# Memory projection steps ahead of the last natural block, x loads ordered across two chunks, and an mLSTM step split off, in a one-core encoder layer

## The chip, the core and the metric

The kernel is one program on one core of a Trainium2 chip. A core has a matrix engine (TensorE, PE in the profile, its weight loads PEld), three engines for elementwise work (VectorE: DVE, ScalarE: ACT, GpSimd: POOL) and SyncE (SP), which here only asks for transfers. Transfers between the chip's memory and the core's on-chip memory run on 16 DMA engines beside them. ScalarE asks for some transfers as well, in its own order of instructions, so one that must wait holds up the work behind it.

The metric is device time in microseconds (us) of one execution, as a median over several.

## The reference

One encoder layer over a sequence of 2048 rows of 1024 numbers, with 256 rows of memory, all in 32-bit floats. Cut to what matters here:

```python
u = rms_norm(h) ; proj = u @ w_in                     # 3600 columns
hy = short_conv(proj[:, :1536])                       # Hyena group, 512 channels
y_hy = group_norm(hyena(hy, spec))                    # two long convolutions by FFT
qk = silu(short_conv(proj[:, 1536:2560]))             # mLSTM group, 4 heads x 128
v, o_pre, gates = proj[:, 2560:3072], proj[:, 3072:3584], proj[:, 3584:]
y_ml = group_norm(sigmoid(o_pre) * (mlstm(qk, v, gates, forward) + mlstm(..., backward)))
h = h + concat(y_hy, y_ml) @ w_out
q = rms_norm(h) @ wq ; k = rms_norm(mem) @ wk ; v = rms_norm(mem) @ wv
h = h + softmax(q k^T / 16) v @ wo                    # 4 heads of 256
h = h + relu(rms_norm(h) @ w1)^2 @ w2 ; return rms_norm(h)
```

The kernel folds the attention's weights into the memory side: for each head it computes keys as (wq of the head) times (the head's k) and values as (the head's v) times (wo of the head), once, ahead of the attention.

## The kernel before, in words

**Tiling.** Wide products are formed as three matmuls of split operands (`mm3`, high and low parts, lines 354, 357 and 358 inside one helper). Splitting means a ScalarE cast for the high part and a VectorE subtraction for the low part (line 365). x is scaled, transposed, split and held for 1024 positions at a time (`xh`, `xl`), as two chunks of 512 positions; `hf` 0 and 1 are the two halves of the sequence.

**Order.** The program is written as generators that are woven. Each `yield` hands the turn over; `chain`, `take`, `among` and `beside_each` set which generator goes next, and `weave` compares the work done in two of them. A scheduler then reorders instructions within each engine by a planner's estimates of readiness, so the text sets the priority and not the exact place.

**The projection.** `sweep(cols, hf, ...)` computes the convolved column tiles (Hyena channels, q, k) transposed, one tile of 256 columns after another. `natural(hf, tiles)` computes v, o and the gates in their natural layout: for each tile of 256 columns (272 with the gates) eight row blocks t of 128 positions, each 24 matmuls, an eviction by ScalarE into a tile `st` and a store asked for by ScalarE into `od` or `vd` (lines 851 and 852). Weights come as `wn` and are split into `wh` and `wl`.

**x.** `x_chunk(c)` makes one chunk of x in four pieces of two row groups: load `xt` (line 518, on SP), scale (DVE, line 507), split (ACT and DVE, line 365). In `prep_x` two such chunks follow each other, and each asks for its first piece when it begins. A `pop` after each row block advances them. The last tile of `natural(1, ...)` starts it at t = 4, since the second half of the row blocks no longer needs the columns of the first chunk.

**The memory side.** `prep_mem` loads the transposed memory and scales it, and starts `raw_stream`, which asks for the weights of wk, wq, wv and wo in the tags `wl` and `wh` (tile `wm`, line 414; two halves of 128 x 1024 words for each) and keeps up to four in flight. `memproj` has eight steps. `project` (line 674) makes a head's k or v from the memory and copies it into `kt` (ACT, line 676). `keys` (line 691, steps 0 to 3) multiplies by wq, copies each piece into a staging tile `o` (ACT, line 681) and stores it as `gd` (asked for by ACT, line 693). `values` (line 703, steps 4 to 7) multiplies by wo, with the store `vw` (line 705). Step n issues `project` n + 1 ahead of `keys` or `values` n.

**The mLSTM.** `states` runs the backward scan and stores the state of each of 16 chunks (line 1154 on PE, `cbd`). `mlstm` then runs the chunks forward: `loads(n)` (q, k, backward state, v; line 1215 and 1138 on SP; rows of gates shuffled by DVE at line 1232), `scores(n)` (PE line 1241; POOL adds masks at line 1248, ACT takes exponentials at line 1250 and DVE multiplies at line 1251), values (PE lines 1279 and 1281), the state's update (PE line 1154, DVE line 1160), and after each second chunk a normalisation over the pair (lines 212 to 220 and 1313). Its tables `rows` (line 1210) take the on-chip memory that x held, so they can be loaded only when the last `natural` has read x.

**Program.** The stretch in question is the end of the projection: sweep columns, `natural(0, (0, 1))`, sweep columns 6 and 7, `natural(0, (2,), p.prep_mem, 2)`, then `take(n, 2)` (two steps of `memproj`), then `beside_each(n, take(m, 6))` (a memory step, an mLSTM step, and so on). All of it is woven with `hyena`, whose last part is back products (lines 943 and 985), inverse steps (lines 177 and 190, which read `zg` and `hy` tiles loaded at lines 927 and 930), and stores. Behind it `attention` starts with 16 transposes (line 1415); the rest of the mLSTM's chunks is woven into it. 

Of the kernel before, what the change touches and what calls it, by code (L numbers as in the profile page):

```python
# [10 lines left out]
F32 = mybir.dt.float32  # L11
# [9 lines left out]
D = 1024  # L21
# [112 lines left out]
class Prog:  # L134
# [270 lines left out]
    def raw_stream(self, pool):  # L405
        q, items = [], list(self.mem_items)

        def load():
            w, n = items.pop(0)
            kt = w.shape[0] // 128  # L410
            t = pool.tile([128, kt, n], F32, tag=("wl", "wh")[len(items) % 2], name="wm", bufs=2)
            for k0 in range(0, kt, kt // 2):
                src = w[128 * k0:128 * k0 + 64 * kt].rearrange("(k p) c -> p k c", p=128)
                self.nc.sync.dma_start(out=t[:, k0:k0 + kt // 2], in_=src)
            q.append(t)

        load()
        load()
        yield
        while q:  # L420
            while items and len(q) < 4:
                load()
            yield q.pop(0)

    def inproj_open(self, es):
# [27 lines left out]
        items += [tr[c] for c in (4, 5, 8, 9)] + nat[:2] + tr[6:8] + nat[2:3]  # L453
        self.items, self.mem_items = items, mem

    def inv_rms(self, dst, src):
        nc, sb, n = self.nc, self.isb, dst.shape[1]
# [60 lines left out]
        self.nc.sync.dma_start(out=t, in_=src[:, 2 * j:2 * j + 2, 512 * c:512 * c + 512])  # L518
# [12 lines left out]
    def x_first(self):  # L531
        nc, sb = self.nc, self.isb
# [91 lines left out]
    def opened(self):  # L624
        self.xes.close()
        return
        yield

    def turned_in(self):
        self.xin.close()  # L630
        return
        yield

    def prep_x(self, hf):
        self.prepq = chain(self.x_chunk(2 * hf), self.x_chunk(2 * hf + 1))

    def prep_mem(self):
        sb = self.isb
        self.memt = [sb.tile([128, 1088], F32, tag="P", name="mt", bufs=2)[:, 0:D].rearrange("p (k t) -> p k t", k=4)
                     for h in range(2)]  # L640
        self.mst = self.raw_stream(sb)
        next(self.mst)

# [15 lines left out]
    def memproj(self):  # L659
# [8 lines left out]
        def project():  # L668
            w = next(self.mst)
            p = self.mm().rearrange("p (k t) -> p k t", k=2)  # L670
            for m in range(2):
                ms = slice(128 * m, 128 * m + 128)
                for k in range(8):
                    mul(p[:, m], w[:, k, ms], mt[k // 4][:, k % 4], start=k == 0, stop=k == 7)  # L674
            t = sb.tile([128, 4, 256], F32, tag="xn", name="kt", bufs=2)[:, 0:2]
            nc.scalar.copy(t, p)
            return t

        def staged(p):
            o = sb.tile([128, 2, 256], F32, tag="st", name="o", bufs=3)  # L680
            nc.scalar.copy(o, p)
            return o

# [142 lines left out]
    def natural(self, hf, tiles, after=None, at=4):  # L826
        nc, a, sb = self.nc, self.a, self.isb
        xh, xl = self.xh, self.xl
        win = a["w_in"][0]
        for c2 in tiles:  # L830
            n = 256 if c2 < 3 else 272
            c0 = 2560 + 256 * c2
            wh, wl = next(self.wst)
# [347 lines left out]
    def mlstm(self, es):  # L1181
# [824 lines left out]
def program(p):  # L2006
    with ExitStack() as ms:
        with ExitStack() as es:
# [11 lines left out]
            weave(s, f, 140, 102, True)  # L2020
            p.gates_open(es)
            n = p.memproj()
            m = p.mlstm(ms)
            with ExitStack() as hs:
                rest = chain(s, p.sweep(range(4, 10), 1, True), p.natural(1, (3, 0, 1, 2), lambda: p.prep_x(0)),
                             p.natural(0, (3,)), among(p.sweep((4, 5, 8, 9), 0, False), p.gates(), 2),
                             among(chain(p.natural(0, (0, 1)), p.sweep((6, 7), 0, False),
                                         p.natural(0, (2,), p.prep_mem, 2)), p.states(), 1),
                             p.turned_in(), take(n, 2), beside_each(n, take(m, 6)))
                weave(rest, p.hyena(hs), 499, 297, True)  # L2030
            for _ in rest:
                pass
# [10 lines left out]
            p.ffn()  # L2043


def among(g, h, every):
    for i, v in enumerate(g):
        yield v
        if i % every == every - 1:
            next(h, None)  # L2050
    for _ in h:
        pass

# [45 lines left out]
```

## Time and profile before

| what | value |
|---|---|
| median of 3 runs | 3133.62 us (3127.82 to 3135.12) |
| the profiled execution | 3131.11 us, span 3129.0 us |
| mean granted TensorE clock | 0.989 |
| HBM read, written | 401.79 MB, 202.41 MB, 193 GB/s over the span |
| x for the first half's sweep is made at | 643 to 692 us |
| `natural(0, (2,))` on TensorE | 1002 to 1036 us |
| first memory projection, last value product | 1036.7 us, 1211.1 us |
| first transposes of the attention | 1233.6 us |
| mLSTM scores begin (chunks 0 to 5) | 1114.5, 1138.4, 1169.7, 1188.4, 1204.5, 1214.9 us |

A row of the profile's timeline gives the start, the duration, the engine and line, the tiles (out<-in), and in brackets how long the engine sat idle ahead of it and what ended that. `PE ... [7.53 <-ACT xh L365]` reads: TensorE did nothing for 7.53 us until ScalarE's cast on line 365 was done. Names that end in q (SPq, ACTq) are an engine's issue of a transfer. A row of windows gives the busy time of each engine in that stretch, the number of instructions, the granted clock of TensorE (1.00 is full), the share of the 16 DMA engines in use, and GB/s.

### The profile page before, as it was taken

How to read it: one execution, taken by the hardware profiler on the slowest of the kernel's cores; microseconds unless marked ns; L12 is line 12 of the kernel's file. 1: busy time of each engine (PE TensorE's matmuls, PEld its weight loads, DVE VectorE, ACT ScalarE, POOL GpSimd, SP SyncE). 2: the span in 40 equal slices, each digit the busy share in tenths (PEclk: the TensorE clock that was granted, in tenths of full speed). 3: DMA queues.
4: the chain of work that ended last, by engine and by line, in shares of the span. 5: the costliest groups of instructions: out<-in, count | busy, mean ns of one | idle time of the engine just before them, and what ended most of it. 6: DMA issues, size and time to landing. Idle time of an engine off the chain costs nothing.

```text
span 3129.0 us, 42943 instructions
## 1 busy us (share of the span) xinstructions
PE 3029.1 (97%) x14257; PEld 2374.5 (76%) x14257; DVE 1964.8 (63%) x3448; ACT 1489.6 (48%) x2907; POOL 1146.9 (37%) x802
## 2 busy tenths in 40 slices
PE   8999999989999898999999999999999999999998
PEld 6655667766677666888887888888888878888876
DVE  7965466446646456777674656657545686555695
ACT  5443366533656225555544455556555533333335
POOL 0122012200113244324141337766456393434493
PEclk9999999999999999999999999999999999999999
DMA  6464767666878897455375657657644574434324
GB/s 212 153 210 163 235 203 220 194 215 216 241 206 249 261 316 245 145 190 186 127 268 186 217 166 243 207 178 231 205 152 153 179 234 142 152 123 152 122 91 172
DMA packets 444101, 607.07 MB, mean 194 GB/s; under 512 B 38494, under 2 KB 248542, under 8 KB 442856
## 3 DMA queue, kind: packets, MB, share of 16 engines
q1 hardware_dynamic: 405988, 546.54, 54.3%
q10 hardware_dynamic: 37892, 57.79, 5.3%
q8 instruction: 113, 1.85, 0.2%
q14 instruction: 108, 0.88, 0.1%
HBM read 401.79 MB, written 202.41 MB: 193 GB/s over the span
## 4 chain that ended last, share of the span: by engine, by line
PE 81%; DMA 7%; DVE 6%; ACT 3%; issue 2%; POOL 1%; SPq 0%; ACTq 0%; DVEq 0%; POOLq 0%
PE mm L354 17%; PE mm L358 17%; PE mm L357 17%; PE hy L358 5%; PE hy L354 5%; PE hy L357 5%; PE hy L177 3%; PE mm L912 1%; PE hy L943 1%; PE hy L985 1%; DMA xt<-in_x_t_dram 1%; DVE bl L1623 1%; PE mm L674 1%; DMA a<-hy 1%; PE mm L703 1%
## 5 line engine op out<-in xcount | busy, mean ns | idle before, releaser
L1623 DVE TENSOR_TENSOR bl<-wr,bh 128x512 fp32r<-128x512 f32 x213 | 239.8, 1132 | 132.5 <-ACT bh L1622 132.3
L1622 ACT CAST ah<-w 128x512 fp32r<-128x512 f32 x284 | 176.9, 624 | 302.5 <-PE hy L357 155.8
L365 DVE TENSOR_TENSOR wl<-wn,wh 128x512 fp32r<-128x512 f32 (+1 forms) x300 | 217.6, 772 | 102.7 <-ACT wh L365 102.4
L354 PE MATMUL mm<-xh,wh 128*128 128x512 f32 x640 | 267.7, 419 | 12.2 <-ACT wh L365 9.1
L990 POOL TENSOR_TENSOR b<-b,a 128x512 f32<-128x512 f32 x64 | 87.0, 1362 | 510.1 <-ACT b L988 320.0
L357 PE MATMUL mm<-xl,wh 128*128 128x512 f32 x640 | 255.8, 400 | 0.7 <-DVE xl L365 0.6
L1622 ACT CAST bh<-wr 128x512 fp32r<-128x512 f32 x232 | 143.8, 622 | 234.6 <-PE mm L358 176.2
L358 PE MATMUL mm<-xh,wl 128*128 128x512 f32 x640 | 255.0, 399 | 0.0
L1623 DVE TENSOR_TENSOR al<-w,ah 128x512 fp32r<-128x512 f32 x236 | 217.6, 922 | 54.9 <-ACT ah L1622 54.9
L358 PE MATMUL mm<-bh,al 128*128 128x512 f32 x576 | 224.1, 392 | 6.8 <-DVE al L1623 4.3
L354 PE MATMUL mm<-bh,ah 128*128 128x512 f32 x576 | 225.7, 392 | 0.5 <-DVE acc L1780 0.4
L357 PE MATMUL mm<-bl,ah 128*128 128x512 f32 x576 | 224.9, 390 | 0.0
L365 ACT CAST wh<-wn 128x512 fp32r<-128x512 f32 (+1 forms) x300 | 167.4, 620 | 110.4 <-PE mm L358 52.1
L357 PE MATMUL mm<-act,wh 128*128 128x512 f32 x512 | 200.5, 393 | 0.8 <-DVE act L365 0.8
L354 PE MATMUL mm<-act,wh 128*128 128x512 f32 x512 | 198.4, 393 | 1.1 <-ACT wh L365 0.9
L358 PE MATMUL mm<-act,wl 128*128 128x512 f32 x512 | 199.1, 392 | 0.3 <-DVE wl L365 0.3
L354 PE MATMUL hy<-bh,ah 128*128 128x512 f32 x448 | 175.2, 391 | 0.0
L357 PE MATMUL hy<-bl,ah 128*128 128x512 f32 x448 | 174.6, 390 | 0.0
L358 PE MATMUL hy<-bh,al 128*128 128x512 f32 x448 | 174.4, 390 | 0.0
L354 PEld LDWEIGHTS mm<-xh,wh 128*128 128x128 f32 x640 | 121.4, 190 | 67.6 <-issue 19.0
L354 PE MATMUL mm<-wh,xh 128*128 128x256 f32 (+1 forms) x512 | 155.7, 305 | 13.0 <-ACT xh L365 10.6
L336 POOL TENSOR_TENSOR b<-b 128x512 f32<-128x512 f32 x32 | 58.3, 1822 | 277.8 <-DVE b L333 137.2
(369 smaller groups left out, 8285.4 us busy)
## 6 DMA issues: line engine op xcount, KB each, us to landing
wr<-hc SPq DMA_DIRECT2D x224, 256.0 KB
w<-in_ff_w_dram SPq DMA_DIRECT2D x172, 256.0 KB
hc<-wn SPq DMA_DIRECT2D x128, 256.0 KB
wn<-in_w_in_dram SPq DMA_DIRECT2D x100, 256.0 KB
hc<-q SPq DMA_DIRECT2D x96, 256.0 KB
fs<-a SPq DMA_DIRECT2D x32, 512.0 KB
a<-fs SPq DMA_DIRECT2D x64, 256.0 KB
a<-zs SPq DMA_DIRECT2D x64, 256.0 KB
```

The lines of the kernel that those rows point to most:

```text
L177: b = self.nc.tensor.matmul(*products[-1], start=True, stop=True)
L336: nc.gpsimd.tensor_tensor(e[1], f, b, ALU.subtract)
L354: first = mm(ps, lh, rh, start=start, stop=False)
L357: mm(ps, lh, rl, start=False, stop=False)
L358: self.last = mm(ps, ll, rh, start=False, stop=stop)
L365: both = (self.nc.scalar.copy(hi, src), self.nc.vector.tensor_tensor(lo, src, hi.bitcast(F32), ALU.subtract))
L674: mul(p[:, m], w[:, k, ms], mt[k // 4][:, k % 4], start=k == 0, stop=k == 7)
L703: mul(p, t[:, m, ms], o_[:, m, ds], start=m == 0, stop=m == 1)
L912: nc.tensor.matmul(pp, dm[:, m], t[:, m], start=True, stop=True)
L990: nc.gpsimd.tensor_tensor(xt, xt, hi[:, m], ALU.mult)
L1622: self.nc.scalar.copy(hi, src)
L1623: eng.tensor_tensor(lo, src, hi.bitcast(F32), ALU.subtract)
```

## The change

Four edits.

1. `x_chunk` becomes `x_chunks`: both chunks of a half run through one list of eight pieces; the first two loads are asked for when the object is made, and the load of piece n + 2 right after piece n is scaled. The last tile of `natural(1, ...)` makes the object at t = 0 and still starts its pieces at t = 4. The first stage uses it as well.
2. Three of the nine turns of `memproj` run ahead of `natural(0, (2,))`: projection 0, then projection 1 with keys 0, then projection 2 with keys 1. `prep_mem` is called in the last sweep column. The weights of `natural(0, (2,))` are made inside `raw_stream` when its fourth weight is handed out, and how many weights it keeps in flight becomes a small table.
3. The memory is scaled in place in its load tiles, `kt` takes a slot of the tag `P`, and the staging tiles `o` alternate between the tags `st` and `cv`.
4. `mlstm` yields once between its first loads and its first scores, and the program takes that step ahead of one more memory step, and then `take(m, 5)` in place of `take(m, 6)`.

```diff
 # raw_stream
         yield
+        n = 0
         while q:
-            while items and len(q) < 4:
+            n += 1
+            if n == 4:
+                self.late_w = iter([self.weights(pool, *self.late_item, kc=2, nbufs=4)])
+            while items and n != 3 and len(q) < {2: 4, 4: 1, 5: 2}.get(n, 4):
                 load()
             yield q.pop(0)
...
-    def x_chunk(self, c):
-        rb = self.spread(self.diagonal(self.rx[:, 4 * c:4 * c + 4]))
-        xs = [self.x_load(c, 0)]
-        for j in range(4):
-            if j < 3:
-                xs.append(self.x_load(c, j + 1))
-            to = slice(2 * j, 2 * j + 2), slice(512 * (c % 2), 512 * (c % 2) + 512)
-            self.scaled(xs.pop(0), 2 * j, self.g_mix, rb, *(t[(slice(None),) + to] for t in (self.xh, self.xl)))
-            yield
+    def x_chunks(self, hf):
+        parts = [(2 * hf + i, j) for i in range(2) for j in range(4)]
+        xs = [self.x_load(*p) for p in parts[:2]]
+
+        def steps():
+            rb = None
+            for n, (c, j) in enumerate(parts):
+                if j == 0:
+                    rb = self.spread(self.diagonal(self.rx[:, 4 * c:4 * c + 4]))
+                to = slice(2 * j, 2 * j + 2), slice(512 * (c % 2), 512 * (c % 2) + 512)
+                self.scaled(xs.pop(0), 2 * j, self.g_mix, rb, *(t[(slice(None),) + to] for t in (self.xh, self.xl)))
+                if n < 6:
+                    xs.append(self.x_load(*parts[n + 2]))
+                yield
+        return steps()
...
     def prep_x(self, hf):
-        self.prepq = chain(self.x_chunk(2 * hf), self.x_chunk(2 * hf + 1))
+        self.prepq = self.x_chunks(hf)
...
-            xs = [load(h) for h in range(2)]
+            xs = self.memt = [load(h) for h in range(2)]
...
-            t = sb.tile([128, 4, 256], F32, tag="xn", name="kt", bufs=2)[:, 0:2]
+            t = sb.tile([128, 1088], F32, tag="P", name="kt", bufs=2)[:, 0:512].rearrange("p (m t) -> p m t", m=2)
...
         def staged(p):
-            o = sb.tile([128, 2, 256], F32, tag="st", name="o", bufs=3)
+            turns[0] += 1
+            if turns[0] % 2:
+                o = sb.tile([128, 2, 256], F32, tag="st", name="o", bufs=3)
+            else:
+                o = sb.tile([128, 1088], F32, tag="cv", name="o", bufs=2)[:, 0:512].rearrange("p (i t) -> p i t", i=2)
...
 # natural
-                if t == at and c2 == tiles[-1] and after is not None:
-                    after()
+                if c2 == tiles[-1] and after is not None:
+                    if t == 0:
+                        nxt = self.x_chunks(0)
+                    if t == at:
+                        self.prepq = nxt
...
 # mlstm
         ld, stores = [loads(0), loads(1)], []
+        yield 1
         scores(0, ld[0])
...
 # program
-            m = p.mlstm(ms)
+            m, st = p.mlstm(ms), p.states()
...
-                             among(chain(p.natural(0, (0, 1)), p.sweep((6, 7), 0, False),
-                                         p.natural(0, (2,), p.prep_mem, 2)), p.states(), 1),
-                             p.turned_in(), take(n, 2), beside_each(n, take(m, 6)))
+                             among(chain(p.natural(0, (0, 1)), p.sweep((6, 7), 0, False, p.prep_mem), take(n, 3),
+                                         p.natural(0, (2,), wst=p.late())), st, 1),
+                             p.turned_in(), take(m, 1), take(n, 1), beside_each(n, take(m, 5)))
```

How this moves instructions, at three places. In each row stand the line, the operation, the tiles (out<-in), the shape and, where a row stands for several instructions, their count. The lines of the changed kernel are some twenty higher.

ScalarE where chunk 1 of x is split (`xh<-xt`) between the evictions `st` of the natural block and their stores `od`; first before:

```order
L503 COPY rb<-mm 128x512
L365 COPY xh<-xt 128x2x512
L851 ACTIVATE st<-mm 128x256
L852 DMA od<-st 128x256
L851 ACTIVATE st<-mm 128x256 x2
L852 DMA od<-st 128x256 x2
L365 COPY xh<-xt 128x2x512
L955 COPY a<-hy 128x512 x2
```

And now:

```order
L507 COPY rb<-mm 128x512
L365 COPY xh<-xt 128x2x512 x2
L871 ACTIVATE st<-mm 128x256 x3
L872 DMA od<-st 128x256 x3
L975 COPY a<-hy 128x512 x2
L365 COPY xh<-xt 128x2x512
```

The second split after the broadcast `rb` stood behind three evictions and three stores; it now stands ahead of them.

TensorE around `natural(0, (2,))` (its matmuls read `wh` and `xh`), first where the block ended before and the memory's projections (`mt,wm`) and keys (`kt,wm`) began:

```order
L358 MATMUL mm<-wh,xl 128x256
L1154 MATMUL hy<-va,kn 128x129 x4
L674 MATMUL mm<-mt,wm 128x256 x14
L1154 MATMUL hy<-va,kn 128x129 x4
L674 MATMUL mm<-mt,wm 128x256 x2
L177 MATMUL hy<-a,e_2618 64x512
L190 MATMUL hy<-a,e_2618 64x512
```

Now, with projection 2 and keys 1 in front of the block (`xt` is the memory, scaled in place):

```order
L685 MATMUL mm<-xt,wm 128x256 x16
L708 MATMUL mm<-kt,wm 128x256
L963 MATMUL hy<-b,em 128x512
L708 MATMUL mm<-kt,wm 128x256 x3
L963 MATMUL hy<-b,em 128x512
L1174 MATMUL hy<-va,kn 128x129 x4
L708 MATMUL mm<-kt,wm 128x256 x12
L354 MATMUL mm<-wh,xh 128x256
L357 MATMUL mm<-wl,xh 128x256
L358 MATMUL mm<-wh,xl 128x256
```

Three projections and two sets of keys moved from behind the natural block to its front, beside the Hyena's back products (`b,em`).

TensorE at the last value products of the memory (`wm,kt`), before, at the end of chunk 3 of the mLSTM (chunk 4 follows, then the transposes):

```order
L703 MATMUL mm<-wm,kt 128x512 x4
L1279 MATMUL hy<-va,rw 128x129
L1281 MATMUL hy<-cbn,rw 128x129
L1279 MATMUL hy<-va,rw 128x129
L1281 MATMUL hy<-cbn,rw 128x129
L1154 MATMUL hy<-ve,kn 128x129 x4
L1241 MATMUL hy<-qn,kk_t 128x128 x4
```

And now, at the end of chunk 0 (chunks 1, 2 and 3 follow, then the transposes):

```order
L1300 MATMUL hy<-va,rw 128x129
L1302 MATMUL hy<-cbn,rw 128x129
L1174 MATMUL hy<-ve,kn 128x129 x4
L720 MATMUL mm<-wm,kt 128x512 x2
L1261 MATMUL hy<-qn,kk_t 128x128 x4
L1300 MATMUL hy<-va,rw 128x129
L1302 MATMUL hy<-cf,rw 128x129
```

The memory's last product stands three chunks earlier in the mLSTM's order than before, and chunk 4 is left to the attention.

More of the change, by code (lines that the diff above doesn't have):

```diff
@@ L452, in inproj_open @@
         items = tr[:4] * 2 + tr[4:] + [nat[c] for c in (3, 0, 1, 2, 3)]
[L453 to L454 removed]
+        items += [tr[c] for c in (4, 5, 8, 9)] + nat[:2] + tr[6:8]
+        self.items, self.mem_items, self.late_item = items, mem, nat[2]
     def inv_rms(self, dst, src):
@@ L627, in opened, with late @@
         yield
+    def late(self):
+        yield next(self.late_w)
     def turned_in(self):
@@ L824, in sweep_out, with natural @@
                 nc.sync.dma_start(out=self.d_kn[t0 + s0:t0 + s0 + rest, cc], in_=st[0:rest, 0])
-    def natural(self, hf, tiles, after=None, at=4):
+    def natural(self, hf, tiles, after=None, at=4, wst=None):
         nc, a, sb = self.nc, self.a, self.isb
@@ L832, in natural @@
             c0 = 2560 + 256 * c2
-            wh, wl = next(self.wst)
+            wh, wl = next(self.wst) if wst is None else next(wst)
             for t in range(8):
@@ L2022, in program @@
             n = p.memproj()
[L2023 removed]
+            m, st = p.mlstm(ms), p.states()
             with ExitStack() as hs:
[L2025 removed]
+                rest = chain(s, p.sweep(range(4, 10), 1, True), p.natural(1, (3, 0, 1, 2), True),
                              p.natural(0, (3,)), among(p.sweep((4, 5, 8, 9), 0, False), p.gates(), 2),
[L2027 to L2029 removed]
+                             among(chain(p.natural(0, (0, 1)), p.sweep((6, 7), 0, False, p.prep_mem), take(n, 3),
+                                         p.natural(0, (2,), wst=p.late())), st, 1),
+                             p.turned_in(), take(m, 1), take(n, 1), beside_each(n, take(m, 5)))
                 weave(rest, p.hyena(hs), 499, 297, True)
@@ L2043, in program, with among @@
             p.ffn()
-def among(g, h, every):
+def among(g, h, every, times=1):
     for i, v in enumerate(g):
@@ L2049, in among @@
         if i % every == every - 1:
-            next(h, None)
+            for _ in range(times):
+                next(h, None)
     for _ in h:
```

3 lines of the change are left out of this document (1 added, 2 removed).

## The prediction

> **What bounds the kernel now.** I read the page's busy table first, then TensorE's waits summed by what ended them, then TensorE's idle time and clock over the three stretches that the change touches.
>
> ```profile
> PE 3029.1 (97%) x14257; PEld 2374.5 (76%) x14257; DVE 1964.8 (63%) x3448; ACT 1489.6 (48%) x2907; POOL 1146.9 (37%) x802
> PE mm L691 <- ACT o L681: 12.9, 2, 10.5
> PE mm L354 <- ACT xh L365: 12.2, 4, 7.5
> PE hy L1279 <- DVE bry L217: 7.5, 2, 5.8
> ```
>
> TensorE is busy for 97%, so about 100 us is all that any reordering can win back. Three waits (total, times, longest) stand near the top of what there is: the memory keys behind their output copies, the natural projection behind the split of x, and the mLSTM's values behind a normalisation. Each belongs to a stage that this change reorders. Elsewhere the same instructions run.
>
> The profiled execution took 3131.11 us (span 3129.0). The median of the three runs is 3133.62, so 2.5 us is added at the end to a sum that is made against the profiled one.
>
> **Part 1, x asked for earlier: -7 us.** Chunk 0 of x is split while the last tile of natural(1) runs; its pieces turn into TensorE work as they come.
>
> ```profile
> 673.77 0.59 PE L354 MATMUL mm<-wh,xh 128*128 128x272 f32 x1 [7.53 <-ACT xh L365]
> 691.19 0.40 PE L354 MATMUL mm<-wh,xh 128*128 128x272 f32 x1 [3.06 <-ACT xh L365]
> 665.47 1.41 DVE L507 SCALAR_TENSOR_TENSOR xt<-xt,par,rb 128x512 f32<-128x512 f32 x2 [4.55 <-DMA xt<-in_x_t_dram]
> 670.05 0.66 ACT L851 ACTIVATE st<-mm 128x256 f32<-128x256 f32 x2 [9.33 <-DMA a<-zg]
> 672.67 1.05 ACT L365 CAST xh<-xt 128x1024 fp32r<-128x1024 f32 x1 [1.96 <-DMA wn<-in_w_in_dram]
> 688.64 1.42 DVE L507 SCALAR_TENSOR_TENSOR xt<-xt,par,rb 128x512 f32<-128x512 f32 x2 [3.12 <-DMA xt<-in_x_t_dram]
> 681.80 0.38 SPq L518 DMA_DIRECT2D xt<-in_x_t_dram  x1
> 670.00:675.00 5.00, 1.23 (x4) 0.95 (x4) 2.12 (x4) 2.19 (x4) 0.00 (x0) 0.50 0.84 286
> ```
>
> The piece is scaled by 665.47 + 1.41 = 666.9, yet ScalarE splits it only at 672.67: an eviction's store stands ahead of it in ScalarE's order, and the row at 670.05 shows 9.33 us lost there. In the new order this split stands ahead of the evictions and their stores. It could then run at about 667 and not 672.67, so some 5 of the 7.53 us go. The last piece was asked for at 681.80 and arrived at 688.64, 6.8 us later, and TensorE idled 3.06 us for it. In the new order its load stands ahead of one gate store, and each load follows its free buffer: 2 of the 3.06 us go. The window's granted clock was 0.50 after the idle 7.53 us, so another 1 to 3 us of slow matmuls may leave with it, and I count none in full. Against that, the first two loads stand where they stood in the queue's order, and the load behind the 665.47 row (asked for at 655.79, 9.7 us) sits in a stretch where the DMA share is 1.02. Sum -7; bounds 0 (the pieces come when they came) and -12 (7.53 + 3.06 and 1.5 of clock).
>
> ```profile
> 655.79 0.39 SPq L518 DMA_DIRECT2D xt<-in_x_t_dram  x1
> 660.00:665.00 5.00, 5.00 (x35) 3.57 (x33) 0.17 (x1) 0.39 (x1) 0.00 (x0) 1.00 1.02 313
> ```
>
> The same edit in the first stage asks for x two pieces ahead where VectorE is the busy engine; I count it at nothing, for VectorE's work covers it, with 1 us at most.
>
> **Part 2, three memory steps ahead of natural(0, 2): -22 us.** Four windows of before: the natural block (1003 to 1036.5), the first memory steps, the next, and the rest up to the last value product.
>
> ```profile
> 1003.00:1036.50 33.50, 32.94 (x229) 28.36 (x228) 19.95 (x37) 18.93 (x31) 8.54 (x9) 1.00 0.73 233
> 1036.50:1080.60 44.10, 33.04 (x155) 26.08 (x154) 15.68 (x45) 5.51 (x12) 16.36 (x14) 0.93 0.93 276
> 1080.60:1120.00 39.40, 31.65 (x123) 23.41 (x124) 13.68 (x43) 12.07 (x33) 8.74 (x6) 0.89 1.04 342
> 1120.00:1212.00 92.00, 90.35 (x427) 63.56 (x427) 52.43 (x170) 37.17 (x124) 41.33 (x31) 0.99 0.84 270
> 1080.60 5.86 PE L691 MATMUL mm<-kt,wm 128*128 128x256 f32 x16 [10.53 <-ACT o L681]
> 1077.10 0.38 ACTq L693 DMA_DIRECT2D gd<-o  x1
> 1077.51 1.28 ACT L1250 ACT_TABLE_LOAD   x1 [20.97 <-DMA qn<-qt]
> 1049.92 5.71 SPq L1210 DMA_DIRECT2D rows<-rows  x5
> 1065.42 0.37 SPq L1215 DMA_DIRECT2D qn<-qt  x1
> ```
>
> The columns are time, busy PE, PE weight loads, DVE, ACT, POOL, granted clock, DMA share and GB/s. Before, this stretch lasts 209 us with 188 busy: 21 us idle, half of it the 10.53 at 1080.60. That one is a chain: ScalarE's store of the first key piece was issued only at 1077.10, 20.97 us after its copy; it waited until the queue's transfers of the rows (from 1049.92) and of q (1065.42) were through. Weighting the busy time by (1 - clock), 0.07 x 33.0 + 0.11 x 31.7 + 0.01 x 90.4 gives some 7 us of slowed matmuls. So the stretch holds about 181 us of warm TensorE work.
>
> After, the work differs. Three mLSTM chunks no longer run inside it: scores, 16 pairs of value products and the update. From the end of chunk 3 before:
>
> ```profile
> 1204.51 1.05 PE L1241 MATMUL hy<-qn,kk_t 128*128 128x128 f32 x8
> 1205.40 0.39 PE L1279 MATMUL hy<-va,rw 128*128 128x129 f32 x2
> 1212.41 1.06 PE L1154 MATMUL hy<-ve,kn 128*128 128x129 f32 x8
> 1214.89 1.16 PE L1241 MATMUL hy<-qn,kk_t 128*128 128x128 f32 x8 [1.42 <-DVE cf L1160]
> 1223.68 0.77 PE L1279 MATMUL hy<-va,rw 128*128 128x129 f32 x2 [5.85 <-DVE bry L217]
> 1231.67 2.09 PE L1154 MATMUL hy<-ve,kn 128*128 128x129 f32 x8 [3.03 <-ACT ht L1293]
> 1233.55 2.55 PE L1415 MATMUL hy<-ident,wn 128*128 128x128 f32 x16
> ```
>
> Scores take 0.9 us (1204.51 to 1205.40), sixteen lines of value products at a pitch of 0.22 another 3.6, the update 0.9: 5.4 us a chunk. So 181 - 3 x 5.4 = 165 us of work is left. The stalls change too. Two projections and keys 0 and 1 now run beside the hyena's back products, before the mLSTM's rows can be loaded at all, so the 10.53 and the 2.63 behind it have no cause left there. The weights come earlier: 10 loads of 128 x 1024 words (0.5 MB) more than before are asked for ahead of the natural block, where the DMA share was 0.84 and 0.73; at the 342 GB/s of the third window they are 15 us of transfer that the saturated windows no longer hold. What is late next: right behind the natural block the rows of chunk 0 load, and in ScalarE's new order the exponentials of chunk 0 stand ahead of the copies of the next keys. From the rows' issue at 1049.92 to the first shuffle took 11 us; four masks are through 6 us later, eight are needed: 22 us in all. One projection (59.4 us for eight, so 7.4) and four short inverse products (0.6 each) cover 10 of them: 12 us of stall. The values' second half loads stand behind those rows on SP too. With 5 us for the first inverse step, whose `a` now follows the natural block more closely, that is 17 us, and 5 for the clock.
>
> ```profile
> 1045.15 0.61 PE L177 MATMUL hy<-a,e 128*64 128x512 f32 x1 [0.53 <-DMA a<-zg]
> L674 PE MATMUL mm<-mt,wm 128*128 128x256 f32 x256 | 59.4, 389 | 2.7 <-ACT o L681 2.7
> 1061.22 0.01 DVE L1232 LOAD_MASK_SELECT rw<-rows  x1 [6.90 <-DMA rows<-rows]
> 1062.12 4.99 POOL L1248 TENSOR_TENSOR rw<-rw,mask 128x512 f32<-128x512 f32 x4 [11.54 <-DVE rw L1232]
> 980.00:1003.00 23.00, 23.00 (x96) 15.51 (x95) 13.97 (x27) 13.26 (x22) 8.22 (x7) 1.00 0.84 243
> ```
>
> 165 + 17 + 5 = 187 us against 209: -22. Bounds: 40 us of stalls and clock (twice the old 21, less the cover) gives 205 and -4; 11 us of them gives 176 and -33.
>
> [...]
>
> **Part 3, the mLSTM a step later: +20 us.** The chunks that leave part 2 are not gone. In the new order only chunk 0 runs beside memory work; chunks 1, 2 and 3 come behind the last value product with nothing else on TensorE, and then the transposes of the attention. Before, that was chunk 4 alone: 1212 to 1233.55, 21.5 us, with 10.4 busy. An uncovered chunk after a normalisation costs, by the updates at 1212.41 and 1231.67, 19.3 us, of which 5.85 is the normalisation; some 3 more was ScalarE waiting for its v. Chunk 2 has a normalisation ahead of it, chunks 1 and 3 have none. I take 16 us for chunk 2 and 10 us each for 1 and 3: 19.3 - 5.85 - 3 = 10.4. So 36 us against 21.5: +14.5. Bounds: three chunks with no wait at all, at the old hole's clock of 0.71 (5.4 / 0.71 = 7.6 each: 23, +1.5), and three times 16 (48, +26.5).
>
> ```profile
> 1212.00:1233.50 21.50, 10.39 (x62) 9.44 (x61) 13.85 (x57) 8.76 (x36) 9.56 (x8) 0.71 0.85 293
> 1216.54 0.70 ACT L1148 ACTIVATE ve<-va,cols 128x129 f32<-128x129 f32 x2 [3.24 <-DMA va<-vd]
> 1240.00:1245.00 5.00, 5.00 (x36) 4.56 (x35) 5.00 (x15) 2.60 (x8) 2.08 (x2) 1.00 0.94 292
> ```
>
> Chunk 4 goes into the attention's weave, where TensorE is full (5.00 of 5.00 in the last row): its 5.4 us come on top, +5.4. The granted clock in the old hole was 0.71. [...]
>
> The remaining edits cost nothing by themselves: the memory scaled in place, the tile of the keys in another pool slot, and the staging copies that alternate between two pool slots keep their counts and shapes. What they change is which buffer a copy waits for, and that lies within part 2's bounds.
>
> **The sum:** -7 - 22 + 14.5 + 5.4 = -9 us: 3122 in the profiled execution's terms, 3124.6 as a median. I say 3124.
>
> **The rivals.** A: *the memory stage stops stalling and the uncovered chunks run tight*: x -5, memory -33, hole +1.5, chunk 4 +5.4 make -31, 3103. For it: DMA was at a share of 1.04 in the window that stalled most, and 15 us of transfer leave it. Against: ScalarE's order behind the natural block, where exponentials precede copies. Chance 0.20. B, **the other side**: *the chunks are left without cover*. Place: behind the last value product. Price: three chunks at 16 us (+26.5), 5.4 in the attention, and -20 from parts 1 and 2 together: +12, 3146. It decides once the hole is longer than 45 us while parts 1 and 2 bring their -29, or the memory stretch longer than 196 with a hole of 36. For it: in the hole's row DVE alone is busy for 13.85 of 21.5 us and the waits are chained. Against: two of the three chunks lack the normalisation. Chance 0.29. C: *a new stall in the old one's place*: the exponentials that precede the key copies bring all of the 10.53 back and some of the DMA's relief is lost; memory -14, x -5, hole +14.5, chunk 4 +5.4: +1, 3134. That x comes no earlier, so that the change doesn't do there what it says, gives -9 + 7 = -2 and 3131, and is counted with C. Chance 0.09. My forecast, -9 with its own range from -18 to 0 (3115 to 3134), has 0.42.
>
> A change under 0.3% (9.4 us) can't be told from none here. A little over half of my own case lies beyond that, since the first stage and the clock of part 1, counted at nothing or in part, can only add: 0.24, and with A 0.44 faster. B and a third of C are slower: 0.32. The rest, 0.24, is the same. The range takes in A with 2 us to spare and a B that is 6 us worse than its price, for a hole of 54.
>
> **What would show it.** Right: the wait of 7.53 behind xh below 3 us; no wait over 5 us of keys behind o; three uncovered chunks in front of the transposes, 30 to 45 us from the last value product; in the memory stretch 176 to 198 us between the end of the sweep and the last value product. Wrong: a memory stretch that stays at 205 or more, a hole over 48, or new waits in the sweeps ahead because the early weights crowd their loads.

## The result, and the profile after

The changed kernel takes 3138.32 us (median of 22 runs, 3132.15 to 3142.8), the kernel before 3133.66 us beside it (22 runs, 3127.1 to 3141.83). The ratio is 1.0013 with a 95% interval of 1.0007 to 1.0018: slower by 2 to 6 us. The forecast was 3124 us and faster, with a range of its own from 3115 to 3134. The time lies outside that, on the other side of no change; only the wider range, which also takes in the rivals (A at 3103, B 6 us above its 3146), holds it.

Single executions of either kernel spread by some 3.5 us (standard deviation). So one trace shows where its time went, and only medians of several say what an edit is worth.

The profiled execution took 3137.02 us with a span of 3135.3, 6.3 more than before. First, six of TensorE's summed waits in the changed kernel (total, times, longest):

```profile
PE mm L354 <- ACT xh L365: 12.8, 3, 8.1
PE mm L685 <- DMA wm<-in_xa_wv_dram: 7.6, 1, 7.6
PE hy L1300 <- DVE bry L217: 5.6, 1, 5.6
PE hy L1436 <- DVE act L365: 5.4, 2, 4.9
PE hy L1547 <- DVE act L365: 2.9, 1, 2.9
PE hy L278 <- ACT b L260: 2.7, 1, 2.7
```

The keys' wait for `o` (12.9 us) is gone, as expected. The wait for `xh` is as long as it was. Four waits are new or longer: for the second half of a `wv` weight, for `act` at two places of the attention, and for `b` in the filters.

Where the 6.3 us came from is read from marks that both traces have: the first or last matmul of a line, whose lines give count, duration, first and last start. Of the changed kernel:

```profile
L932 PE MATMUL mm<-a,dm x128: 590/592/697, 413.7 to 1017.0; 128*128 128x512 f32 x128
L1108 PE MATMUL hy<-ident,ends x2: 270/271/272, 765.5 to 768.7; 128*1 128x128 f32 x2
L720 PE MATMUL mm<-wm,kt x64: 592/592/697, 1137.1 to 1187.5; 128*128 128x512 f32 x64
L1261 PE MATMUL hy<-qn,kk_t x128: 272/275/422, 1159.9 to 1545.5; 128*128 128x128 f32 x128
L1436 PE MATMUL hy<-ident,wn x128: 270/272/477, 1220.4 to 1692.6; 128*128 128x128 f32 x128
L1607 PE MATMUL hy<-ssum,ones x8: 592/592/697, 1419.4 to 1874.9; 128*128 128x512 f32 x8
```

| mark | before | after | gained or lost since the mark above |
|---|---|---|---|
| first Hyena product (lines 912, 932) | 409.5 | 413.7 | +4.2 |
| the gates' `ends` (1088, 1108), behind the x stage | 759.0 | 765.5 | +2.3 |
| last value product (703, 720) | 1211.1 | 1187.5 | -30.1 |
| first transposes of the attention (1415, 1436) | 1233.6 | 1220.4 | +10.4 |
| last `ssum` product, end of the attention (1586, 1607) | 1870.1 | 1874.9 | +18.0 |
| end of the span | 3129.0 | 3135.3 | +1.5 |

The memory stage won 30 us, more than the forecast's 22. (Counted as the prediction did, from the end of the sweep, it took 180.5 us, 1007.0 to 1187.5, in place of 209.) Nearly all of it was given back in the next 700 us: 10.4 in the stretch without memory work, 18.0 in the attention. The first two marks had lost 6.5 more.

Two windows of the changed kernel show that stretch and the start of the attention (time, busy PE, PEld, DVE, ACT, POOL, granted clock, DMA share, GB/s), and its timeline the idle times of TensorE there:

```profile
1188.00:1220.40 32.40, 21.69 (x145) 20.16 (x143) 23.58 (x88) 19.27 (x85) 17.79 (x15) 0.79 0.82 269
1220.40:1300.00 79.60, 73.06 (x380) 62.52 (x381) 62.26 (x154) 43.85 (x123) 27.84 (x20) 0.96 0.53 169
```

```profile
1203.55 0.77 PE L1300 MATMUL hy<-va,rw 128*128 128x129 f32 x2 [5.61 <-DVE bry L217]
1220.41 0.66 PE L1436 MATMUL hy<-ident,wn 128*128 128x128 f32 x4 [0.70 <-DVE cf L1180]
1227.57 1.12 PE L1436 MATMUL hy<-ident,wn 128*128 128x128 f32 x4 [4.89 <-DVE act L365]
1347.58 1.07 PE L1547 MATMUL hy<-ident,e 128*128 128x128 f32 x4 [2.90 <-DVE act L365]
```

Three chunks took 32.4 us there, 10.8 each; one of them paid 5.61 for a normalisation. In the attention TensorE is idle for 15.3 us against 5.8 before (its length from the first transposes to the last `ssum` product, less the busy time), and the clock of 0.96 in the first 80 us means by estimate some 3 us of slowed matmuls ((1 - 0.96) x 73.06 busy us; before it was 0.99 with 77.43 busy, so under 1 us).

VectorE's and ScalarE's timeline at the 4.89 us gap:

```profile
1220.67 1.13 DVE L1316 SCALAR_TENSOR_TENSOR ht<-hy,den,ht 128x128 f32<-128x128 f32 x4
1225.18 0.17 DVE L215 TENSOR_SCALAR hy<-brm 128x8 int32<-128x8 int32 x1 [3.38 <-ACT brm L212]
1226.82 0.69 DVE L365 TENSOR_TENSOR act<-hy,act 128x512 fp32r<-128x512 f32 x1
1224.85 0.30 ACT L212 ACTIVATE brm<-ss,eps 128x8 f32<-128x8 f32 x1
```

With chunk 3 as the last one ahead of the attention, the normalisation of chunks 2 and 3 stands in VectorE's order ahead of the split of the attention's first operand. VectorE waited 3.38 us for it (line 215), and TensorE 4.89 us for the split. This stall isn't new, it has moved. Before, the same normalisation stood ahead of the values of chunk 4: VectorE waited 4.44 us for it at 1220.53, and TensorE the 5.85 us of the row at 1223.68 that the prediction shows, in the stretch in front of the attention.

### The profile page after: what moved, and what is told of

Its sections match the earlier page's. It is cut to its first block, busy times and chain, and to the rows that moved or that the text cites. A ratio compares the mean times of both kernels' runs of the same rounds, so it can differ in the third digit from the quotient of the medians.

```text
span 3135.3 us, 42950 instructions
## 1 busy us (share of the span) xinstructions
PE 3034.6 (97%) x14257; PEld 2379.4 (76%) x14257; DVE 1970.0 (63%) x3448; ACT 1484.0 (47%) x2905; POOL 1144.3 (36%) x802
## 4 chain that ended last, share of the span: by engine, by line
PE 83%; DVE 6%; DMA 5%; issue 2%; ACT 2%; POOL 2%; SPq 0%; ACTq 0%; DVEq 0%; POOLq 0%
PE mm L354 17%; PE mm L358 17%; PE mm L357 17%; PE hy L358 5%; PE hy L354 5%; PE hy L357 5%; PE hy L177 3%; PE mm L932 2%; PE mm L685 2%; PE hy L1005 2%; PE hy L963 2%; DMA xt<-in_x_t_dram 1%; PE mm L720 1%; PE hy L1174 1%; PE hy L1300 1%
```

## The experiments

The change has three independent groups of edits: x in the first stage (F), x in the second (X), the memory and mLSTM edits (M, with chunk 4 left to the attention, the deferral). Outside the stages that its edits reach, the order on every engine is that of before in e2 and that of the change in e3, but for single rows, so their times can be set side by side. In e1 it isn't quite: at the start of the attention (1223 to 1253 us) and near 1370, some of its loads, casts and matmuls stand in another order than in the change. Medians are of 11 or 12 runs; the ratio is to the kernel before, which ran beside them.

**e1: both x edits undone.**

```diff
...
-        self.prepq = self.x_chunks(hf)
+        self.prepq = chain(self.x_chunk(2 * hf), self.x_chunk(2 * hf + 1))
...
-                             ... p.natural(1, (3, 0, 1, 2), True),
+                             ... p.natural(1, (3, 0, 1, 2), lambda: p.prep_x(0)),
```

> The change with both x edits undone: x_chunk in pairs again, started at t = 4, everything else as changed. Theory (the x edits lose time: by the marks of the two traces 4.2 us in the first stage and 2.3 us where x is split for the last time): about 6.5 us under the changed kernel, 2 us under the kernel before, near 3131.5; the first hyena rows (line 409 before) back within 1 us of before, the wait for xh at about 7.5. Rival (those offsets are run to run spread, and the loss lies in the attention): 3138, as the change.

Measured: 3138.77 us, ratio 1.0014 (1.0004 to 1.0025). In the trace the first stage is back (the first Hyena product 1.5 us ahead of before) and the wait for `xh` is 7.59; and yet the median did not fall: the rival's 3138 came, not the 3131.5 of the theory. With the memory part changed, taking both x edits away gains nothing.

**e2: the kernel before with both x edits alone.** The diff is the change's own part 1.

> The kernel before with the two x edits alone. Theory: slower by 6.5 us, near 3140, with the same offsets of +4 in the first stage and +2 in the second as the change. Rival (the x edits cost nothing, or gain when the rest is unchanged): 3134 or less.

Measured: 3138.51, ratio 1.0017 (1.0008 to 1.0026), so slower, as the theory had it; but in its trace only 0.8 us had gathered by the first Hyena product and 1.1 by the mark behind the x stage, and the rest came later, where the order is that of before but for single rows. This and e1 don't add up to one price for the x edits.

**e3: the x edit undone in the first stage only.**

```diff
...
     def prep_x(self, hf):
-        self.prepq = self.x_chunks(hf)
+        self.prepq = chain(self.x_chunk(2 * hf), self.x_chunk(2 * hf + 1))
```

> The change with the x edit undone in the first stage only (prep_x there uses x_chunk, the last tile of natural(1) keeps x_chunks). Theory: 4 us under the change, near 3134, with the first stage as before and the x stage as in the change (wait for xh of 8). Rival: the first stage differs by spread alone, 3138.

Measured: 3133.59, ratio 1.0003 (0.9994 to 1.0011): 4.7 us under the change, as expected. The wait for `xh` is 6.72 at its longest, where 8 was expected.

**e4: e1 with chunk 4 ahead of the attention again.**

```diff
-                             p.turned_in(), take(m, 1), take(n, 1), beside_each(n, take(m, 5)))
+                             p.turned_in(), take(m, 1), take(n, 1), beside_each(n, take(m, 6)))
```

> As e1, with take(m, 6) in place of take(m, 5), so that chunk 4 comes ahead of the attention again, uncovered. Theory (a chunk is dearer without cover than beside the attention): the stretch from the last value product to the transposes grows by 10 to 17 us, the attention shrinks by 5.4 for the work and by its first wait of 4.9, so e1 plus 0 to 7 us. Rival (the attention's loss of 18 us is all chunk 4 and the order it starts in): e1 minus 3 to 8 us.

Measured: 3137.41, ratio 1.0011 (1.0002 to 1.0020), 1.4 under e1. By its trace the last value product to the transposes grew to 53.0 us (1184.8 to 1237.8, e1 35.7), and the attention to its last `ssum` product shrank to 639.8 from 656.0. What moves between the two places, some 16 to 17 us, is the same on both sides; neither theory's sign is borne out.

**e5 and e6: the x edits one by one, on the kernel before.**

```diff
 # e5: the sweep's prep_x(1) makes x_chunks(1); natural(1) keeps the pair of x_chunk
-lambda: p.prep_x(1)
+lambda: p.prep_x_all(1)
...
 # e6: natural(1) makes x_chunks(0) at t = 0; the sweep keeps the pair of x_chunk
-                if t == at and c2 == tiles[-1] and after is not None:
-                    after()
+                if t in (0, at) and c2 == tiles[-1] and after is not None:
+                    after(t)
```

> The kernel before with the x edit in the first stage alone. Theory (this edit alone costs the 4.7 us by which the change stands above e3): 3138, with the first stage's offsets of the change (line 409's first product 4 us later). Rival (the 4.7 is an interplay with the memory part further down): 3134.

> The kernel before with the x edit in the last tile of natural(1) alone. Theory (from e1 and e3 it is worth 5 us, from all five kernels by additive parts 2.7): 3128 to 3131, the wait for xh at about 6 instead of 7.5. Rival (it gains only together with the memory part): 3134 or more.

Measured: e5 3136.99, ratio 1.0005 (0.9996 to 1.0014); e6 3133.47, ratio 0.9996 (0.9987 to 1.0004). By its median F alone costs some 3 us, less than the 4.7 that were expected, and its interval takes in no cost at all; its first Hyena product comes 3.2 us later than before. X alone is worth nothing that shows, where 2.7 to 5 us were expected: its longest wait for `xh` is 7.19.

Where F loses time is seen in the traces. Up to the first Hyena product TensorE is idle for 20.8 to 22.0 us in the three kernels with F (the change, e2, e5) and for 17.9 to 19.5 in the other eleven. With the new order of the x loads the scheduler also moved two other loads, of 0.5 MB each (`c_win`, line 296), in among the stores of `hy<-st`. SyncE's issues in the changed kernel:

```profile
85.35 1.63 SPq L522 DMA_DIRECT2D xt<-in_x_t_dram  x2
87.04 0.45 SPq L296 DMA_DIRECT2D a<-in_c_win_dram  x1
87.59 0.88 SPq L811 DMA_DIRECT2D hy<-st  x2
88.90 0.95 SPq L296 DMA_DIRECT2D a<-in_c_win_dram  x1
90.31 10.55 SPq L811 DMA_DIRECT2D hy<-st  x3
```

And before, where both follow at 113.54; with it VectorE's copy that needs a store's buffer, before and then after:

```profile
87.06 12.18 SPq L794 DMA_DIRECT2D hy<-st  x5
113.54 1.01 SPq L296 DMA_DIRECT2D a<-in_c_win_dram  x2
93.30 0.69 DVE L207 COPY st<-mm 126x512 f32<-126x512 f32 x1 [2.72 <-DMA hy<-st]
```

```profile
96.00 0.69 DVE L207 COPY st<-mm 126x512 f32<-126x512 f32 x1 [4.29 <-PE mm L808]
99.07 2.08 PE L278 MATMUL hy<-b,fw 128*128 128x512 f32 x2 [2.67 <-ACT b L260]
```

The copy came 2.7 us later (96.00 for 93.30), and what stands behind it on VectorE too. After, the profile names a matmul as what ended its wait; in e5, with the same order, it names the store (4.14 us, at 96.15). TensorE's wait at line 278 was then 2.67 us, and 2.53 in e5, 1.76 in e2, and 0.66 to 1.64 in the eleven kernels with the old first stage. Behind it the granted clock from 95 to 105 us was 0.67 in the change and 0.83 in e5, but 1.00 in e2 and before; the two matmuls behind that wait took 2.08 us in the change and e5, and 1.12 in e2 and before. By estimate from these rows the change lost 1.6 us there by the longer wait (2.67 for 1.11 before) and 2.4 by slowed matmuls ((1 - 0.67) x 7.3 busy us), together about the 4.2 by which its first Hyena product is late. That the two loads slow those stores was not tried by itself.

**e7: e3 with two turns of the memory part ahead, not three.**

```diff
-            if n == 4:
+            if n == 3:
...
-            while items and n != 3 and len(q) < {2: 4, 4: 1, 5: 2}.get(n, 4):
+            while items and n != 2 and len(q) < {3: 1}.get(n, 4):
...
-   p.sweep((6, 7), 0, False, p.prep_mem), take(n, 3),
+   p.sweep((6, 7), 0, False, p.prep_mem), take(n, 2),
```

> As e3, with two turns of the memory part ahead of the natural block and not three (projection 0, then projection 1 and keys 0; the weights of the block made one weight earlier). Theory (a turn ahead saves stalls but takes cover from an mLSTM chunk, and the two nearly cancel): the last value product 5 to 10 us later than e3, the stretch to the transposes shorter by up to as much, the whole within 5 us of e3. Rival (the cover is not what sets the uncovered stretch, since chunk 0 starts late anyway): stretch as long as in e3 (33), whole 5 to 10 us slower than e3.

Measured: 3132.97, ratio 0.9995 (0.9984 to 1.0006), so equal to e3. Last value product 3.7 us later than in e3 (1185.5), transposes 1222.0: 36.5 us between them against 33.2. The stretch did not shrink, as the rival had it, but the whole did not grow either. Two turns ahead or three make no difference that shows. Its first scores came 20.5 us sooner than in e3 (1133.6 for 1154.1), and the attention still began 7 us later.

**e8: e3 with all copies `o` in the tag `st`.**

```diff
-            if turns[0] % 2:
+            if True:
```

> As e3, with all staging copies o in the tag st, as before. Theory (the stalls behind o went because the steps were moved, not because the staging alternates): no wait for o above 3 us, whole within 3 us of e3. Rival (three slots of one tag, shared with the natural block's evictions, bring the stall back): a wait for o of 5 to 10 us, 3139 to 3144.

Measured: 3136.62, ratio 1.0006 (0.9997 to 1.0015). The longest wait for `o` is 0.9 us: the alternating slots are not what removed the stall. The whole stands 3 us above e3, at the edge of what was expected, and about two standard errors of the difference.

**e9: the kernel before with the mLSTM edit alone** (the step split, chunk 4 left to the attention).

```diff
         ld, stores = [loads(0), loads(1)], []
+        yield 1
         scores(0, ld[0])
...
-                             p.turned_in(), take(n, 2), beside_each(n, take(m, 6)))
+                             p.turned_in(), take(n, 1), take(m, 1), take(n, 1), beside_each(n, take(m, 5)))
```

> The kernel before with the mLSTM edit alone: the step split behind its loads, and take(m, 5), so that chunk 4 goes to the attention. Theory (the attention begins with transposes of chunks 0 to 3, so with chunk 3 last its normalisation, store and load stand uncovered in front of the attention; this and chunk 4's own work cost 15 us or more there, and a chunk fewer uncovered saves about as much): a wait of 3 to 6 us for `act` early in the attention, the attention 12 to 19 us longer, the whole within 4 us of before. Rival (the attention's 18 us in the change come from the memory part, its later key and value stores): attention longer by 5 to 6 us only, and the whole 5 to 10 us faster than before.

Measured: 3134.38, ratio 1.0006 (0.9997 to 1.0015). Its marks:

```profile
L703 PE MATMUL mm<-wm,kt x64: 592/592/697, 1152.7 to 1206.3; 128*128 128x512 f32 x64
L1416 PE MATMUL hy<-ident,wn x128: 270/273/476, 1214.8 to 1694.2; 128*128 128x128 f32 x128
L1587 PE MATMUL hy<-ssum,ones x8: 592/592/697, 1418.0 to 1878.3; 128*128 128x512 f32 x8
PE hy L1416 <- DVE act L365: 5.0, 4, 3.6
```

The transposes came 18.8 us earlier than before, and the attention was 27 us longer (663.5 against 636.5; 12 to 19 were expected), with the memory steps not moved ahead of the natural block. So the loss in the attention comes with the deferral, and here with the split step: leaving chunk 4 to the attention is no gain, even where it empties the stretch in front.

**e10: e3 with chunk 4 ahead again** (`take(m, 6)`, as in e4).

> As e3 (the change with the first stage's x edit undone), with take(m, 6): chunk 4 ahead of the attention, behind four uncovered chunks. Theory: the stretch from the last value product to the transposes 50 to 55 us in place of 33, the attention within 4 us of before, no wait for `act` at its start, the whole 0 to 5 us above e3. Rival (deferral is a loss): 5 us or more under e3.

Measured: 3135.20, ratio 1.0002 (0.9993 to 1.0011). Its marks, and the window between them:

```profile
L730 PE MATMUL mm<-wm,kt x64: 592/592/697, 1133.0 to 1183.5; 128*128 128x512 f32 x64
L1446 PE MATMUL hy<-ident,wn x128: 270/273/421, 1234.4 to 1691.4; 128*128 128x128 f32 x128
L1271 PE MATMUL hy<-qn,kk_t x128: 272/275/474, 1155.9 to 1528.2; 128*128 128x128 f32 x128
1184.00:1234.40 50.40, 30.45 (x194) 28.18 (x193) 35.20 (x135) 27.25 (x118) 25.96 (x22) 0.77 0.68 220
```

All came as expected, and this is the clearest of the twelve. The memory's last value product came 27.6 us sooner than before (1183.5 for 1211.1), and the attention began 0.8 us later (1234.4 for 1233.6). The attention is within 2 us of before (638.4 to its last `ssum` product, before 636.5), with no long wait for `act`. All that the memory steps won was lost in front of the attention, by chunks that run one behind the other with no cover: 50.9 us for four. In TensorE's idle time it is seen best. It fell from 24.3 to 14.7 us in the memory stage (behind the x stage, to the last value product) and rose from 11.1 to 19.9 in the stretch behind it; the busy times of the two together are 439.2 and 440.9. Against e3 it also gives the price of the deferral: 17.7 us less in the stretch, 16.3 more in the attention.

**e11 and e12: the other way round.** If the chain of chunks leads to the attention, it should begin sooner. Both are e6 with the memory part behind the natural block, as before:

```diff
 # e11
-  p.turned_in(), take(n, 2), beside_each(n, take(m, 6)))
+  p.turned_in(), take(n, 1), beside_each(n, take(m, 6)))
 # e12, with the yield of e9 ahead of scores(0)
+  p.turned_in(), take(n, 1), take(m, 1), beside_each(n, take(m, 6)))
```

> The kernel before with the second stage's x edit, and take(n, 1) in place of take(n, 2): the memory part stays behind the natural block, and the mLSTM begins one memory turn sooner. Theory (the way to the attention leads from the natural block's end over the rows and the chain of chunks, and memory work is only its cover; so the chain has to begin sooner, not the memory work): first scores 10 us or more ahead of e6's 1114, the stretch from the last value product to the transposes down from 22 to 8 to 15, the whole 5 to 12 us under before. Rival (chunk 0 waits for its loads whatever its place in the order): scores within 4 us of e6, whole within 3 us of before or slower, with the new wait in front of the first scores.

> As e11, with the mLSTM's first step split behind its loads, so that the loads of chunks 0 and 1 are asked for a memory turn ahead of the first scores, and take(m, 6) behind it. Theory: as e11, with the first scores up to 8 us later than there but fewer stalls in front of them; transposes 5 to 12 us ahead of before's 1233.6. Rival: the loads push back the weights on the same queue, a wait of 5 us or more for wm or for o, and the whole no faster than before.

Measured: e11 3132.66, ratio 0.9990 (0.9981 to 0.9999), the only one of the twelve with an interval below 1, by 0.3 to 6 us, which one in twelve may reach by chance; e12 3136.78, ratio 1.0002 (0.9989 to 1.0015), no gain. In e11:

```profile
L1263 PE MATMUL hy<-qn,kk_t x128: 272/275/377, 1085.1 to 1522.9; 128*128 128x128 f32 x128
L725 PE MATMUL mm<-wm,kt x64: 592/592/697, 1148.5 to 1206.6; 128*128 128x512 f32 x64
L1437 PE MATMUL hy<-ident,wn x128: 270/273/421, 1229.3 to 1686.8; 128*128 128x128 f32 x128
PE mm L713 <- ACT o L703: 15.2, 4, 10.6
```

The first scores came 29 us sooner (1085.1 for 1114.5), the transposes 4.3 us sooner, and the stretch was still 22.7 us. The old 10.6 us wait for `o` is back and does not hinder that. The whole gained less than the 5 to 12 us that the theory gave, so an earlier start of the chain is not by itself an earlier attention. e12's first scores came at 1105.7 and its update of a chunk waited 8.8 us in front of the attention.

## Why the prediction was wrong

A least squares fit of four additive parts to the means of ten kernels (before, the change, e1 to e6, e9, e10) gives F +2.9, X -1.5, the memory steps +2.1 and the deferral +0.6, each with a standard error of 0.7 us. It doesn't fit well (e2 is 1.8 and e3 1.7 standard errors off, with four parts for ten kernels), so these are sizes and no more. Their sum is +4.1; by the means the change stands some 4 us above before.

By the marks of the two traces, two terms of the sum failed by 13 us each: x with its first stage (-7 forecast, 6.5 lost by the second mark) and chunk 4 in the attention (+5.4 forecast, +18.0). The other two came out better than forecast, by 8 and by 4, and 1.5 more were lost behind the attention.

- **x asked for earlier, -7 us, first stage at nothing.** Wrong. The prediction took 5 us off the 7.53 because the split would stand ahead of the evictions. In the changed kernel the split that had stood until 672.67 did run early, at 667.34, and the gap moved to the next piece: a load asked for at 669.99 behind two weight loads, scaled only from 680.50.

```profile
665.93 3.14 SPq L394 DMA_DIRECT2D wn<-in_w_in_dram  x2
669.99 0.37 SPq L522 DMA_DIRECT2D xt<-in_x_t_dram  x1
680.50 1.41 DVE L511 SCALAR_TENSOR_TENSOR xt<-xt,par,rb 128x512 f32<-128x512 f32 x2 [6.18 <-DMA xt<-in_x_t_dram]
683.04 0.59 PE L354 MATMUL mm<-wh,xh 128*128 128x272 f32 x1 [8.14 <-ACT xh L365]
```

  The gap before was 7.53 at one piece and is 8.14 at the next; the 3.06 behind it is 2.91. The failing steps are "so some 5 of the 7.53 us go", which looked at one piece and not at the next, and "each load follows its free buffer". The buffer of that next load was free at 660.92 (the last read of its old piece), and the load came 9.1 us later, in SyncE's order behind loads of the Hyena and of weights; before it came 6.2 us behind its buffer (656.92 to 663.08). So it was asked for no sooner than before, and it then took 10.5 us to arrive, at a DMA share of 1.05 and then 0.83. And the first stage, costed at nothing because VectorE covers it, cost about 3: the edit reordered loads there that the prediction had not looked at.
- **The memory steps, -22 us.** The mechanism was right and the term too small: -30.1 in this trace. The stall for `o` went, and the only large one in its place was the second half of `wv`, which the text had named: 7.61 us behind the rows and q loads. The 12 us that the prediction put behind ScalarE's exponentials did not show as a wait for `kt` or `o`. The 342 GB/s at which it priced the ten loads at 15 us are a mean over 39 us, though: in 5 us of the same window of before (1100 to 1105) the transfers ran at 406, at a DMA share of 1.05.

```profile
1112.43 2.93 PE L685 MATMUL mm<-xt,wm 128*128 128x256 f32 x6 [7.61 <-DMA wm<-in_xa_wv_dram]
```

- **The stretch in front of the attention, +14.5.** Right: 36 us forecast, 32.9 measured from mark to mark (1187.5 to 1220.4), 22.5 before.
- **Chunk 4 in the attention, +5.4.** Wrong, and with x the step that failed: "its 5.4 us come on top". It counted only TensorE's work of the chunk. The attention took 18.0 us more: 9.5 of new idle time (15.3 against 5.8) and 8.4 of busy time, which holds the chunk's own work and slowed matmuls (by the estimate above some 2 us more of them in the first 80 us than before). e9 shows the loss without the memory steps moved, and e10 against e3 that the deferral only moves 16 to 18 us from the stretch into the attention. That the normalisation of chunks 2 and 3 in VectorE's order is the cause of the first gap is read from the trace. The other runs agree: the longest wait of the transposes for `act` there is 3.4 to 4.9 us in the six kernels that leave chunk 4 to the attention, and 1.3 to 2.1 in the eight that don't.
- **The sum.** The terms were made as if the memory work were on the way to the attention. In the program's order the attention waits for chunks 0 to 3, these for the rows, and these for the natural block's end, which the change put 48 us later (its last matmul is at 1083.6; before, at 1035.4). The first scores moved by 45.4 (1114.5 to 1159.9). The memory steps are the chain's cover: doing them sooner leaves the chain uncovered, which e10 shows. That the start of the chain decides when the attention begins is not shown: in e7 the first scores came 20 us sooner than in e3 and the transposes 7 us later, and in e11 they came 29 us sooner than before and the transposes only 4. Rival B said where the loss would be, and priced it 5 us too high per chunk (16 for the 10.8 measured); its place was partly right, but the larger part stood in the attention, where no rival had put it. Of the prediction's signs of being right only the wait for `xh` failed; the hole (32.9 us), the keys' wait for `o` and the memory stretch (180.5 us) came as it said, since none of the signs looked at the attention.

What stays open is the interplay: the x edits cost 5 us on the kernel before (e2) and nothing on the changed memory part (e1 against the change), though F alone cost 4.7 there (e3 against the change). Behind the x stage e2 has the order of before but for single rows; e1's differs from the change's at the start of the attention. No run here tells why the price differs, nor how far apart two kernels with the same order would lie.

## What to carry to other kernels

Before moving work ahead of a stage, follow back what the next stage waits for: if a serial chain is left between the two, the moved work was its cover, and the idle time that goes from one place comes back in the other. When a step of such a chain is deferred, look at what it used to wait for: the first instructions of the next stage wait for it now. Sum the deferred step's waits with its work. With a scheduler in between, compare the order of transfers in every stage that calls an edited helper, also where the edit looks idle.

## What was not expected of the hardware

The three uncovered chunks ran at a granted clock of 0.79 and four at 0.77 (in e10), with TensorE busy for 67 and 60% of those windows. In the changed kernel the clock was 1.00 from 1188 to 1197.9 us, where no gap was longer than 0.7 us, 0.77 from there to 1203.5, which is the gap of 5.61, 0.50 from 1203.5 to 1213 and 0.90 from there to 1220.4. So its low mean was made in that one gap and the 17 us behind it; what lowers the clock was not tried by itself. Between single executions of one kernel the times spread by 3.3 to 4.1 us (standard deviation of the change, e1, e2, e3 and e4), as much as most of the edits here are worth.
